# A decoder step on one core: the sample's closing sums, projection banks, cached-memory key steps and decode pacing

## The chip, the cores and the metric

One program runs on one core of a Trainium2 chip, in one launch. The metric is the device time of an execution in microseconds (us). The engines named below are TensorE (PE, with its weight loads PEld), VectorE (DVE), ScalarE (ACT), GpSimd (POOL) and SyncE (SP). POOL, ACT and SP also issue DMA transfers, each from its own queue.

## What is computed

One inference step of a decoder layer for two groups of rows that share the weights: a prompt of 1024 rows and a sample of 8 rows, one per sequence, width 1024, all in fp32. The sample attends to 8192 cached positions per sequence through a page table. In short:

```python
q, k, v, logf, u, z = mixer_inputs(rmsnorm(xs, g_mix), w_in, b_f, g_sgu_v)
att = fox_sample(q, k, v, logf, cache_k, cache_v, cache_logf, page_table)
xs = xs + merge_heads(att, sgu_sample(u, z, w_s, b_s), g_att_out, g_sgu_out, w_o)
xs = xs + cross_attend(rmsnorm(xs, g_cross), cache_mem_k, cache_mem_v, w_cq, w_co)
f, conv_s = conv_ffn(rmsnorm(xs, g_ffn), state_conv, w_up, conv_w, conv_b, w_down)
y_sample = rmsnorm(xs + f, g_final)
```

The prompt goes through the same layer with causal attention over its own rows, cross-attention into 256 memory tokens, and the same gated feed-forward block (width 2816, twice for gate and value). Outputs are both groups' results and the new keys, values, gates, memory keys and values and convolution states.

## The kernel before

**Two programs in one.** `prompt()` and `sample()` are Python generators that record instructions. `prompt()` yields an estimate of TensorE time after each piece of work. The loop at the end of `build` adds these estimates to `acc` and takes the next step of `sample()` whenever `acc` reaches the figure that `PACE` holds for the current phase. The phases of the prompt are p1 (projections), att0 and att1 (attention of the two halves of the rows), mid0 and mid1 (output projection and cross-attention of a half), ffn0 and ffn1 (its feed-forward block). While the sample is in its decode part, the figure is the prompt phase's; behind decode it is that of `rest`. After the recording, a scheduler with a timeline of its own orders the instructions of each engine; each engine then runs its queue strictly in that order and waits on semaphores.

**The prompt.** Its products are written as three fp32r matmuls each (high times high, high times low, low times high; lines 246 to 248, 410 to 412, 973 to 975). Weights come in 512 KB loads on SP's queue, and ACT and DVE split each into its high and low part (lines 209 and 210). Product tiles take PSUM banks from two rings, `ba` (four banks) and `bb` (two), in turns through `BK()`. In the feed-forward block DVE empties a bank with lines 1194 and 1195, and line 1226 adds a down-projection's product to the residual.

**The sample.** Each of its matrix products has 8 rows, so its weights are the moving operand and four products stand side by side in the 32-column groups of one bank (line 258, `sample_mm`; lines 1371, 1568, 1614 and 1653 for values, memory values, up- and down-projection). A product with a selection matrix (`selS`, lines 1465 and 1666) then sums the four groups into 8 rows. It has two banks of its own, `ms` and `dv`, one each, and four buffers `kv` of 1 MB, filled on POOL's queue, for everything that it loads: cached keys and values (lines 1306 and 1365), weights (1474, 1610, 1648) and cached memory (1531, 1564).

**The rest of the sample behind decode** (`sample_rest`): closing the attention, then `sample_proj` with `w_o`, a norm, `sample_proj` with `w_cq`, whose result goes through a DRAM tensor `q2s_d` and comes back broadcast to all partitions; the key steps of the cached memory, one for each of eight sequences (two multiplications, line 1535, and a reduction, line 1536, on DVE); softmax; the memory's values; `sample_proj` with `w_co`; the up-projection (22 steps of 1 MB), the down-projection (11 steps of 1 MB into `ys`, one `dv` and one `ms` bank), the closing sums (line 1666, in banks from `BK()`), the final norm and the store of `o_ys`.

**Order by hand.** `behind(e)` records an instruction so that the scheduler issues it after the newest prompt instruction of engine `e` at that point; decode's DVE and PE steps use it (lines 1310 and 1369).

Of the kernel before, what the change touches and what calls it, by code (L numbers as in the profile page):

```python
# [11 lines left out]
AF = mybir.ActivationFunctionType  # L12
ALU = mybir.AluOpType
AX = mybir.AxisListType
PSUM = bass.MemoryType.PSUM
ENG = mybir.EngineType
DRAM = bass.MemoryType.DRAM

P = 128
# [10 lines left out]
FF = 2816  # L30
NF = FF // P
NPAGE = 64
EPS = 1e-6
NEG = -1e30
UW = 1024
# [37 lines left out]
KS = 2  # L73
BKQ = 1
LA = (2, 2)
PACE = {'p1': 7.0, 'att0': 20.0, 'mid0': 8.0, 'ffn0': 8.5, 'att1': 15.0, 'mid1': 6.8, 'ffn1': 2.5, 'rest': 2.9}


def build(nc, tc, ctx, a, phases=None):
# [13 lines left out]
    def nm(s):  # L93
        cnt[0] += 1
        return f"{s}_{cnt[0]}"
# [13 lines left out]
    def KV():  # L109
        return dpool.tile([P, 2048], F32, tag="kv", bufs=NKV, name=nm("kv"))  # L110

    def sm(shape, tag, bufs=2, dt=F32):
        return small.tile(shape, dt, tag=tag, bufs=bufs, name=nm(tag))

    def BA():
        return psum.tile([P, 512], F32, tag="ba", bufs=4, name=nm("ba"))

    def BB():
        return psum.tile([P, 512], F32, tag="bb", bufs=2 + MB, name=nm("bb"))
# [3 lines left out]
    def BK():  # L123
        turn_[0] += 1
        return BB() if turn_[0] % BR == BR - 1 else BA()
# [3 lines left out]
    def MS():  # L129
        return BB() if MB else psum.tile([P, 512], F32, tag="ms", bufs=1, name=nm("ms"))  # L130

    def DV():
        return psum.tile([P, 512], F32, tag="dv", bufs=1, name=nm("dv"))

    def D2(n=512, dt=F32):
        return dpool.tile([P, 512], dt, tag="d2", bufs=5, name=nm("d2"))[:, :n]
# [5 lines left out]
    mmul = nc.tensor.matmul  # L142
# [12 lines left out]
    selS = cp[:, C_SELS : C_SELS + 8]  # L155
# [6 lines left out]
    epsb = const.tile([P, 1], F32, tag="epsb", name="epsb")  # L162
    nc.vector.memset(epsb, EPS)
    warm = const.tile([P, 1], F32, tag="warm", name="warm")
# [28 lines left out]
    def rstd_of(ssq, n, width, tag):  # L193

        p = ssq.shape[0]
        r = sm([P, width], tag + "r", 2)[:p]
        nc.vector.tensor_scalar(r, ssq, 1.0 / n, EPS, op0=ALU.mult, op1=ALU.add)
        nc.gpsimd.tensor_tensor(r, r, mhalf[:p, :width], op=ALU.pow)
# [54 lines left out]
    def sample_mm(ps, raw, kk, xT, n, off=0):  # L253

        for q in range(2):
            k = kk * 2 + q
            j = k % 4
            mmul(
                ps[32 * j : 32 * j + 32, :n],
                xT[:, k, :],  # L260
                raw[:, q, off : off + n],
                start=(k < 4),
                stop=(k >= 4),
                tile_position=(0, 32 * j),
            )
# [43 lines left out]
    def p1(early):  # L309
# [25 lines left out]
        def stats(hf):  # L335
# [9 lines left out]
            for dst, m in ((rstd8, 64.0), (rstd, 1.0)):  # L345
                v = sm([P, 4], "xv", 2)
                nc.vector.tensor_scalar(v, ssx[:, c], m / D, m * EPS, op0=ALU.mult, op1=ALU.add)
                nc.gpsimd.tensor_tensor(dst[:, c], v, mhalf[:, :4], op=ALU.pow)
# [898 lines left out]
    bgs, acc, phase = [], [0.0], ["p1", None]  # L1247

    def behind(e):

        return tc.issue_after(last[e]) if e in last else nullcontext()
# [208 lines left out]
    def sample_out(n, ps, fin):  # L1460
        t = D2()
        nc.scalar.activation(t, ps, AF.Copy)
        yield 1
        ps2 = MS()
        mmul(ps2[:8, :], selS, t, start=True, stop=True)
        fin(n, ps2[:8, :])

    def sample_proj(w, xT, fin):
        for n in range(2):
            ps = MS()  # L1470
            for kk in range(4):
                if kk % 2 == 0:
                    raw = KV().rearrange("p (k n) -> p k n", n=512)
                    nc.gpsimd.dma_start(raw, w[kk * 256 : (kk + 2) * 256, n * 512 : (n + 1) * 512].rearrange("(k p) n -> p k n", p=P))
                    yield 1
                sample_mm(ps, raw[:, (kk % 2) * 2 : (kk % 2) * 2 + 2, :], kk, xT, 512)
            yield from sample_out(n, ps, fin)

    def sample_rest(xs):
        yield 1  # L1480
# [31 lines left out]
        def add(n, ps):  # L1512
            nc.vector.tensor_tensor(xs[n], ps, xs[n], op=ALU.add)

        yield from sample_proj(a["w_o"], xsT, add)
        yield from sample_norm(xs, gp[:, G_CROSS : G_CROSS + 8], xsT)
        q2s = pair("s")

        def toq(n, ps):
            nc.vector.tensor_scalar(q2s[n], ps, 1.0 / 16, None, op0=ALU.mult)  # L1520
            nc.sync.dma_start(q2s_d[:, n * 512 : (n + 1) * 512], q2s[n])

        yield from sample_proj(a["w_cq"], xsT, toq)

        sS = sm([P, 2, 8, 4], "sS", 1)
        for b in range(8):
            qb = [D2(), D2()]
            for n in range(2):
                nc.gpsimd.dma_start(qb[n], q2s_d[b : b + 1, n * 512 : (n + 1) * 512].broadcast_to((P, 512)))
            kv = KV()  # L1530
            nc.gpsimd.dma_start(kv.rearrange("p (a c) -> p a c", c=D), a["cmk"][b].rearrange("(a p) c -> p a c", p=P))
            kvv = kv.rearrange("p (a c) -> p a c", c=D)
            for n in range(2):
                kn = kvv[:, :, n * 512 : (n + 1) * 512]
                nc.vector.tensor_tensor(kn, kn, qb[n].unsqueeze(1).broadcast_to((P, 2, 512)), op=ALU.mult)
            nc.vector.tensor_reduce(sS[:, :, b, :], kv.rearrange("p (a h d) -> p a h d", a=2, h=4), axis=AX.X, op=ALU.add)
            yield 1
        yield 1
        tr = MS()
        for mt in range(2):  # L1540
# [21 lines left out]
        for b in range(8):  # L1562
            kv = KV().rearrange("p (a c) -> p a c", c=D)
# [11 lines left out]
            op=ALU.mult,  # L1575
# [3 lines left out]
        for n in range(2):  # L1579
            ps = MS()  # L1580
# [3 lines left out]
        sample_T(y, ones[:, 0:8], xsT)  # L1584
        yield 1
        yield from sample_proj(a["w_co"], xsT, add)
        yield from sample_norm(xs, gp[:, G_FFN : G_FFN + 8], xsT)

# [14 lines left out]
        for f4 in range(11):  # L1603
            ps = DV()
            for q in range(2):
# [6 lines left out]
                for k in range(8):  # L1612
# [5 lines left out]
                        start=(k < 4),  # L1618
                        stop=(k >= 4),
# [3 lines left out]
            t = D2()  # L1623
# [21 lines left out]
        ys = [DV(), MS()]  # L1645
        for f2 in range(0, NF, 2):
            raw = KV().rearrange("p (f d) -> p f d", f=2)
            nc.gpsimd.dma_start(raw, a["w_down"][f2 * P : (f2 + 2) * P, :].rearrange("(f p) d -> p f d", p=P))
            for q in range(2):
                f = f2 + q  # L1650
                j = f % 4
                for n in range(2):
                    mmul(
                        ys[n][32 * j : 32 * j + 32, :],
                        g[:, f * 8 : f * 8 + 32],
                        raw[:, q, n * 512 : (n + 1) * 512],
                        start=(f < 4),
                        stop=(f >= NF - 4),
                        tile_position=(0, 32 * j),
                    )  # L1660
            yield 1
        for n in range(2):
            t = D2()
            nc.scalar.activation(t, ys[n], AF.Copy)
            ps = BK()
            mmul(ps[:8, :], selS, t, start=True, stop=True)
            add(n, ps[:8, :])
        r = rms8(xs)
        for n in range(2):
# [85 lines left out]
    def sample():  # L1755
        yield from decode()
        phase[1] = "rest"
        yield from sample_rest(pair("dec"))
# [4 lines left out]
    for t in prompt():  # L1763
        ins = nc.cur_bb.bb.instructions
        for e in (ENG.DVE, ENG.PE):
            for i in range(len(ins) - 1, max(seen, len(ins) - 400) - 1, -1):
                if ins[i].engine == e:
                    last[e] = ins[i]
                    break
        acc[0] += t  # L1770
        most = int(t / PACE[phase[1] or phase[0]]) + 1
        while bgs and not held[0] and most and acc[0] >= PACE[phase[1] or phase[0]]:
            most -= 1
            acc[0] -= PACE[phase[1] or phase[0]]
            if next(bgs[0], None) is None:
                bgs.pop()
        seen = len(nc.cur_bb.bb.instructions)
    for _ in bgs.pop() if bgs else ():
        pass
# [90 lines left out]
```

## Time and profile before

| | |
|---|---|
| median of 3 runs | 1930.2 us (1928.2 to 1940.83) |
| the profiled execution | 1933.38 us, of which span 1931.6 us |
| mean granted TensorE clock in it | 0.972 of full speed |
| DMA | 517.07 MB, mean 268 GB/s over the span |
| cached keys and values, POOL's queue | 128 + 128 loads of 1 MB |
| PE busy / DVE busy in 1500 to 1600 | 100.00 / 54.17 us |
| PE busy / DVE busy in 1600 to 1700 | 92.47 / 73.93 us |

The profile is one execution, recorded by the hardware profiler. All positions in time are microseconds from the span's start. Busy times of PE are modelled, since matmuls are pipelined: distances from start to start tell more than lengths. A matmul of plain fp32 (the sample's) appears as two records, one of fp32r as one. "Waits" give, for an idle engine, what it waited for by the last semaphore. The times of decode in it: its last value products stand at about 1490, and the rest of the sample runs from there to 1866, the prompt to the end.

### The profile page before, as it was taken

To read this page: it belongs to the slowest core of one execution; us is meant where nothing else is said; L and a number is where in the kernel's file an instruction comes from. 1 tells how busy PE (TensorE), PEld (TensorE's weight loads), DVE (VectorE), ACT (ScalarE), POOL (GpSimd) and SP (SyncE) were. 2 spreads that over 40 slices of the span, in tenths; PEclk is the share of its full clock that TensorE was granted. 3 is DMA by queue.
4 is the path that set the end of the run, shared out by engine and by line. 5 is a ranking of instruction groups with operands and counts; after the bars stand their busy time and mean duration, and the time that the engine had idled before them with its cause. 6 is when DMAs were issued, how large, how long until landed. Compare 5 with 4: busy or idle time off the path is not lost.

```text
span 1931.6 us, 24224 instructions
## 1 busy us (share of the span) xinstructions
PE 1821.0 (94%) x9255; PEld 1300.7 (67%) x9255; DVE 1403.6 (73%) x1662; ACT 760.8 (39%) x1435; POOL 475.3 (25%) x429
## 2 busy tenths in 40 slices
PE   8999989778898999999999999998999998999798
PEld 5987667555676667777767776675665776667456
DVE  4888668777687786989989899888764459553134
ACT  5332356566632535333333233335353333332122
POOL 1322232322123232223331323343312012101200
PEclk9999999899999999999999999998999998999899
DMA  8877988744496875869787889888769467767841
GB/s 322 288 240 274 332 316 294 255 154 144 158 358 242 317 291 196 304 258 347 283 310 289 312 294 362 322 325 308 282 259 344 163 205 252 290 174 290 332 156 65
DMA packets 156372, 517.07 MB, mean 268 GB/s; under 512 B 20168, under 2 KB 41928, under 8 KB 123488
## 3 DMA queue, kind: packets, MB, share of 16 engines
q0 software_dynamic: 56400, 339.04, 47.1%
q1 hardware_dynamic: 92944, 163.89, 24.4%
q10 hardware_dynamic: 6912, 12.59, 1.7%
q8 instruction: 73, 1.20, 0.2%
q14 instruction: 43, 0.35, 0.1%
HBM read 493.63 MB, written 21.84 MB: 267 GB/s over the span
## 4 chain that ended last, share of the span: by engine, by line
PE 64%; DVE 7%; DMA 4%; ACT 3%; issue 2%; POOL 0%; DVEq 0%; POOLq 0%; ACTq 0%; SPq 0%
PE ba L246 9%; PE ba L247 9%; PE ba L248 9%; PE bb L246 5%; PE bb L247 5%; PE bb L248 5%; PE dv L1371 5%; DMA kv<-cache_k,kidx 2%; DVE kv L1312 1%; DMA kv<-w_down 1%; DVE s L1316 1%; PE ba L973 1%; PE ba L975 1%; PE ba L974 1%; PE dv L1614 1%
## 5 line engine op out<-in xcount | busy, mean ns | idle before, releaser
L209 ACT ACTIVATE wh<-wr 128x1024 fp32r<-128x1024 f32 (+2 forms) x220 | 228.8, 1044 | 474.9 <-PE ba L247 147.1
L210 DVE TENSOR_TENSOR wl<-wr,wh 128x1024 fp32r<-128x1024 f32 (+2 forms) x220 | 262.4, 1200 | 146.0 <-PE ba L248 60.6
L1312 DVE TENSOR_TENSOR kv<-kv,d 128x2048 f32<-128x2048 f32 (+1 forms) x139 | 292.4, 2114 | 33.9 <-DMA kv<-cache_k,kidx 31.9
L1306 POOL DMA_INDIRECT kv<-cache_k,kidx x128 | 179.6, 1403 | 556.0 <-DVE s L1316 251.0
L1316 DVE TENSOR_REDUCE s<-kv 128x32 f32<-128x2048 f32 (+1 forms) x139 | 292.1, 2106 | 0.6
L1365 POOL DMA_INDIRECT kv<-cache_v,kidx x128 | 176.2, 1376 | 419.1 <-PE dv L1371 162.4
L246 PE MATMUL ba<-wh,u 128*128 128x512 f32 (+1 forms) x591 | 224.2, 381 | 0.0
L247 PE MATMUL ba<-wl,u 128*128 128x512 f32 (+1 forms) x591 | 223.8, 379 | 0.0
L248 PE MATMUL ba<-wh,u 128*128 128x512 f32 (+1 forms) x591 | 220.8, 378 | 0.5 <-DVE u L210 0.5
L246 PE MATMUL ba<-u,wh 128*128 128x512 f32 (+2 forms) x528 | 206.7, 392 | 1.3 <-DVE u L213 1.2
L247 PE MATMUL ba<-u,wh 128*128 128x512 f32 (+2 forms) x528 | 207.3, 393 | 0.0
L248 PE MATMUL ba<-u,wl 128*128 128x512 f32 (+2 forms) x528 | 206.3, 391 | 0.0
L1371 PE MATMUL dv<-kv,s 128*32 128x512 f32 x1024 | 135.8, 609 | 4.8 <-DMA kv<-cache_v,kidx 4.8
L246 PE MATMUL bb<-u,wh 128*128 128x512 f32 (+2 forms) x336 | 134.9, 401 | 2.2 <-DVE u L213 2.2
L247 PE MATMUL bb<-u,wh 128*128 128x512 f32 (+2 forms) x336 | 133.3, 397 | 2.5 <-DVE u L213 2.5
L248 PE MATMUL bb<-u,wl 128*128 128x512 f32 (+2 forms) x336 | 132.6, 395 | 0.0
L246 PEld LDWEIGHTS ba<-wh,u 128*128 128x128 f32 x591 | 111.3, 188 | 30.1 <-issue 7.1
L248 PEld LDWEIGHTS ba<-wh,u 128*128 128x128 f32 x591 | 110.8, 188 | 26.7 <-issue 4.6
L247 PEld LDWEIGHTS ba<-wl,u 128*128 128x128 f32 x591 | 111.3, 188 | 22.7 <-issue 2.1
L246 PEld LDWEIGHTS ba<-u,wh 128*128 128x128 f32 x528 | 100.3, 190 | 32.9 <-issue 8.0
L247 PEld LDWEIGHTS ba<-u,wh 128*128 128x128 f32 x528 | 100.5, 190 | 31.9 <-issue 11.3
L248 PEld LDWEIGHTS ba<-u,wl 128*128 128x128 f32 x528 | 100.4, 190 | 28.6 <-issue 8.9
(419 smaller groups left out, 3124.1 us busy)
## 6 DMA issues: line engine op xcount, KB each, us to landing
wr<-w_up SPq DMA_DIRECT2D x88, 512.0 KB
kv<-w_up POOLq DMA_DIRECT2D x22, 1024.0 KB
wr<-w_down SPq DMA_DIRECT2D x40, 512.0 KB
kv<-w_down POOLq DMA_DIRECT2D x11, 1024.0 KB
wr<-w_in SPq DMA_DIRECT2D x16, 512.0 KB
wr<-w_o SPq DMA_DIRECT2D x16, 512.0 KB
wr<-w_cq SPq DMA_DIRECT2D x16, 512.0 KB
wr<-w_co SPq DMA_DIRECT2D x16, 512.0 KB
```

The lines of the kernel that those rows point to most:

```text
L209: nc.scalar.activation(h, src, AF.Copy)
L210: nc.vector.tensor_tensor(l, src, h.bitcast(F32), op=ALU.subtract)
L246: mmul(out, sh, mh, start=(i == 0), stop=False)
L247: mmul(out, sh, ml, start=False, stop=False)
L248: mmul(out, sl, mh, start=False, stop=(i == n - 1))
L973: mmul(pss[i], mh[k][:, tb], wh, start=(k == korder[0]), stop=False)
L974: mmul(pss[i], mh[k][:, tb], wl, start=False, stop=False)
L1306: nc.gpsimd.indirect_dma_start(kv, None, a["cache_k"], off(kidx[:, b, ch : ch + 1]))
L1312: nc.vector.tensor_tensor(kvv[:, i : i + m, :], kvv[:, i : i + m, :], qb.unsqueeze(1).broadcast_to((P, m, 512)), op=ALU.mult)
L1316: nc.vector.tensor_reduce(s[:, ch * 4 + i : ch * 4 + i + m, :].rearrange("p k h -> p (k h)"), kvv[:, i : i + m, :].rearrange("p k (h d) -> ...
L1365: nc.gpsimd.indirect_dma_start(kv, None, a["cache_v"], off(kidx[:, b, ch : ch + 1]))
L1371: mmul(dv[32 * j : 32 * j + 32, :], s[:, ch * 4 : ch * 4 + 4, :].rearrange("p k h -> p (k h)"), kvv[:, j, :], start=(ch == 0), stop=(ch == ...
```

## The change

- `PACE`: mid0 8.0 to 8.3, ffn0 8.5 to 8.8, mid1 6.8 to 7.2 (decode's steps are taken less often there), rest 2.9 to 2 (the rest's steps more often).
- `sample_proj`: the two halves of the columns take `dv` and `ms` in turns instead of `ms` twice; both halves' products come first, then both sums, each in the bank that its half had. One step fewer is yielded for each projection.
- The key steps of cached memory: DVE's part is recorded inside `behind(ENG.DVE)`, and the reduction over both halves of the memory is written as two.
- The closing sums: both banks `ys` are copied out first, and the sums take `dv` and `ms` instead of banks from `BK()`.
- The loop's step may yield a weight `w`, which takes `w` times the pace; every yield is 1 here (`CMK` = 1), so this does nothing as it stands.

```diff
-PACE = {'p1': 7.0, 'att0': 20.0, 'mid0': 8.0, 'ffn0': 8.5, 'att1': 15.0, 'mid1': 6.8, 'ffn1': 2.5, 'rest': 2.9}
+PACE = {'p1': 7.0, 'att0': 20.0, 'mid0': 8.3, 'ffn0': 8.8, 'att1': 15.0, 'mid1': 7.2, 'ffn1': 2.5, 'rest': 2}
...
     def sample_out(n, ps, fin):
         t = D2()
         nc.scalar.activation(t, ps, AF.Copy)
         yield 1
-        ps2 = MS()
+        ps2 = (DV, MS)[n]()
         mmul(ps2[:8, :], selS, t, start=True, stop=True)
         fin(n, ps2[:8, :])
 
     def sample_proj(w, xT, fin):
+        outs = []
         for n in range(2):
-            ps = MS()
+            ps = (DV, MS)[n]()
             for kk in range(4):
...
                 sample_mm(ps, raw[:, (kk % 2) * 2 : (kk % 2) * 2 + 2, :], kk, xT, 512)
-            yield from sample_out(n, ps, fin)
+            outs.append(sample_out(n, ps, fin))
+            next(outs[n])
+        for o in outs:
+            yield from o
+        yield 1
...
-            for n in range(2):
-                kn = kvv[:, :, n * 512 : (n + 1) * 512]
-                nc.vector.tensor_tensor(kn, kn, qb[n].unsqueeze(1).broadcast_to((P, 2, 512)), op=ALU.mult)
-            nc.vector.tensor_reduce(sS[:, :, b, :], kv.rearrange("p (a h d) -> p a h d", a=2, h=4), axis=AX.X, op=ALU.add)
-            yield 1
+            with behind(ENG.DVE):
+                for n in range(2):
+                    kn = kvv[:, :, n * 512 : (n + 1) * 512]
+                    nc.vector.tensor_tensor(kn, kn, qb[n].unsqueeze(1).broadcast_to((P, 2, 512)), op=ALU.mult)
+                for i in range(2):
+                    nc.vector.tensor_reduce(sS[:, i, b, :], kvv[:, i, :].rearrange("p (h d) -> p h d", h=4), axis=AX.X, op=ALU.add)
+            yield CMK
...
+        ts = [D2(), D2()]
         for n in range(2):
-            t = D2()
-            nc.scalar.activation(t, ys[n], AF.Copy)
-            ps = BK()
-            mmul(ps[:8, :], selS, t, start=True, stop=True)
+            nc.scalar.activation(ts[n], ys[n], AF.Copy)
+        for n in range(2):
+            ps = (DV, MS)[n]()
+            mmul(ps[:8, :], selS, ts[n], start=True, stop=True)
             add(n, ps[:8, :])
...
-            if next(bgs[0], None) is None:
+            w = next(bgs[0], None)
+            if w is None:
                 bgs.pop()
+            else:
+                acc[0] -= (w - 1) * PACE[phase[1] or phase[0]]
```

More of the change, by code (lines that the diff above doesn't have):

```diff
@@ L32 @@
 NPAGE = 64
+CMK = 1
 EPS = 1e-6
```

## The prediction

> **What bounds the kernel now.** I read the page's parts 1 and 4 first, then stages, then TensorE's own order in time.
>
> ```profile
> PE 1821.0 (94%) x9255; PEld 1300.7 (67%) x9255; DVE 1403.6 (73%) x1662; ACT 760.8 (39%) x1435; POOL 475.3 (25%) x429
> ...
> PE 64%; DVE 7%; DMA 4%; ACT 3%; issue 2%; POOL 0%; DVEq 0%; POOLq 0%; ACTq 0%; SPq 0%
> ```
>
> TensorE is busy 94% of the span and carries 64% of the chain of waits. Both kernels issue the same matmuls, so the change can only move time in which TensorE stands still, or the cost of switching between prompt and sample. I therefore looked for places where no prompt matmul runs. The stages around the largest one (columns: length, then busy time of PE, PEld, DVE, ACT, POOL, then granted clock, DMA share, GB/s):
>
> ```profile
> 1755.20:1805.00 49.80, 49.80 (x374) 35.02 (x373) 15.05 (x19) 13.11 (x20) 8.76 (x13) 1.00 0.90 325
> 1805.00:1855.80 50.80, 35.55 (x219) 12.68 (x218) 4.21 (x8) 5.87 (x11) 9.27 (x13) 0.80 0.82 320
> 1855.80:1906.60 50.80, 50.80 (x218) 40.42 (x218) 27.93 (x43) 17.76 (x32) 0.56 (x1) 1.00 0.16 54
> 1906.60:1931.60 25.00, 17.26 (x75) 13.66 (x73) 12.34 (x23) 6.20 (x17) 2.17 (x4) 0.92 0.21 85
> ```
>
> In 1805 to 1855.8 PE is busy 35.55 of 50.80 us at a granted clock of 0.80, while DMA moves 320 GB/s. The 50.8 us behind it have PE full and DMA nearly idle at 54 GB/s. PE's order in time shows what that hole is (start, length, instructions merged; brackets: idle before and its releaser):
>
> ```profile
> 1804.67 0.40 PE L248 MATMUL ba<-u,wl 128*128 128x512 f32 x1
> 1805.00 1.07 PE L1614 MATMUL dv<-kv,xsT 128*32 128x256 f32 x16
> 1806.00 1.06 PE L1629 MATMUL ms<-cp,d 128*128 128x8 f32 x8
> 1806.99 1.07 PE L1614 MATMUL dv<-kv,xsT 128*32 128x256 f32 x16
> ...
> 1825.26 1.96 PE L1653 MATMUL dv<-kv,d 128*32 128x512 f32 x8 [2.53 <-issue]
> 1826.94 1.96 PE L1653 MATMUL ms<-kv,d 128*32 128x512 f32 x8
> ...
> 1834.63 1.06 PE L1653 MATMUL dv<-kv,d 128*32 128x512 f32 x4 [3.39 <-DMA kv<-w_down]
> ...
> 1849.28 1.93 PE L1653 MATMUL dv<-kv,d 128*32 128x512 f32 x4 [2.49 <-DMA kv<-w_down]
> ...
> 1854.86 1.02 PE L1666 MATMUL bb<-d,cp 128*8 128x512 f32 x2 [0.76 <-ACT d L1664]
> ...
> 1855.81 0.50 PE L246 MATMUL bb<-u,wh 128*128 128x512 f32 x1
> ```
>
> From 1804.67 to 1855.81 there is only sample work: the end of its up-projection, all of its down-projection, its first closing sum (L1666), and directly behind that sum the prompt's next matmul. The sum's bank comes from BK, the prompt's own ring. In the old program order 109 sample matmuls stand in one run here; elsewhere the longest run is 20. The rows name loads of `w_down` as what PE waits for.
>
> **Part 1, the closing sums.** The hole is 1855.81 − 1804.67 − 0.23 (one prompt matmul) = 50.9 us. The work in it, start to start at full rate: 6 blocks L1614 at 1.00, 4 of L1629 at 0.99, 11 steps L1653 at 1.68, the sum 0.95: 6.0 + 4.0 + 18.5 + 0.95 = 29.4. So 21.5 us are waits and half-rate matmuls. With the sums in DV and MS, the new program order has no run over 20 sample matmuls: the last up steps, a block of 16 and seven blocks of 4 in the down-projection, and the sums stand between prompt matmuls. That costs switching:
>
> ```profile
> 1481.81 0.39 PE L246 MATMUL ba<-u,wh 128*128 128x512 f32 x1
> 1482.13 1.06 PE L1371 MATMUL dv<-kv,s 128*32 128x512 f32 x8
> 1483.13 0.51 PE L247 MATMUL ba<-u,wh 128*128 128x512 f32 x1
> 1483.47 0.40 PE L248 MATMUL ba<-u,wl 128*128 128x512 f32 x1
> ```
>
> A block of 8 takes 1483.47 − 1481.81 − 2 × 0.23 = 1.20 us, of which 0.86 is its own (16 take 0.86 more), so 0.34 a switch. The new order has about 11 more switches in this stretch: 3.7 us. Do the loads keep up? The chain shows the steady spacing ahead of the hole, and SyncE the sample's last store:
>
> ```profile
> 1792.66 1.00 PE dv L1614 x16
> ...
> 1800.94 1.00 PE dv L1614 x16
> ...
> 1864.69 0.99 SPq L1674 DMA_DIRECT2D o_ys<-dec  x2
> ```
>
> Two sample steps of 1 MB each stand every 8.3 us, in the old order to 1805 and in the new one to the end of the up-projection. A `kv` buffer is reused four steps later, so a load has two spacings less its own pair (16.6 − 3) = 14 us of PE work to hide in, and at that spacing PE was full from 1755 to 1805. In the hole, at 1.0 to 1.7 us a step, it had 4 to 7. In the new down-projection the order leaves it 14 us or more. Over 1755 to 1907 DMA moved 49.8 × 325 + 50.8 × 320 + 50.8 × 54 = 35.2 MB, 233 GB/s when spread; so I take no wait. Part 1: −21.5 + 3.7 = **−17.8 us**; bounds −21.5 (no switch cost) and −4 (14 us of the waits stay). From the first closing sum to the sample's last store it took 1865.7 − 1854.86 = 10.8 us; behind the second sum the new order still has 82 prompt matmuls, 18.9 us, so this ending stays covered. A sum now waits for ACT's copy out of its own bank (0.76 us in the row of L1666), with prompt matmuls queued behind it; the new order puts some ahead of it too, so I take none of that.
>
> **Part 2, key steps of cached memory.** Sixteen multiplications stay; eight reductions become sixteen halves. DVE's rows in 1575 to 1645, and the nearest half-size reduction:
>
> ```profile
> L1535 DVE TENSOR_TENSOR kv<-kv,d 128x1024 f32<-128x1024 f32 x16 | 19.3, 1219 | 5.2 <-DMA d<-q2s_d 5.2
> L1536 DVE TENSOR_REDUCE sS<-kv 128x8 f32<-128x2048 f32 x8 | 18.2, 2280 | 0.0
> L210 DVE TENSOR_TENSOR wl<-wr,wh 128x1024 fp32r<-128x1024 f32 x10 | 12.2, 1220 | 2.3 <-PE ba L248 2.3
> L1194 DVE SCALAR_TENSOR_TENSOR t<-ba,gp,t 128x511 f32<-128x511 f32 x5 | 3.7, 745 | 0.4 <-ACT hlast L1193 0.4
> L1195 DVE SCALAR_TENSOR_TENSOR t<-ba,gp,t 128x510 f32<-128x510 f32 x5 | 3.7, 740 | 0.0
> L1201 DVE TENSOR_TENSOR t<-t,t 128x512 f32<-128x512 f32 x3 | 2.1, 687 | 0.0
> L210 DVE TENSOR_TENSOR u<-t,u 128x512 fp32r<-128x512 f32 x3 | 2.1, 687 | 0.0
> L1197 DVE TENSOR_TENSOR t<-t,fix 128x2 f32<-128x2 f32 x8 | 1.2, 151 | 0.0
> ...
> L1316 DVE TENSOR_REDUCE s<-kv 128x16 f32<-128x1024 f32 x22 | 26.3, 1208 | 0.1
> ```
>
> The split itself: 8 × (2 × 1.208 − 2.280) = 1.1 us of DVE. [...] Today these steps cost PE a stall:
>
> ```profile
> 1620.87 0.40 PE L248 MATMUL ba<-wh,u 128*128 128x512 f32 x1
> 1628.23 0.77 PE L246 MATMUL bb<-wh,u 128*128 128x512 f32 x1 [6.97 <-DVE t L1197]
> 1628.80 0.63 PE L247 MATMUL bb<-wl,u 128*128 128x512 f32 x1
> ```
>
> PE waits 7 us for a bank that DVE empties late, then runs at half rate (0.57 instead of 0.23 apart). Counting DVE work from the first key step to what PE needs: in the old order up to a `wl`, 16 × 1.219 + 7 × 2.280 of sample and 8 × 1.220 + 7 × (0.745 + 0.740 + 0.151) + 3 × 0.687 + 2 × 0.687 of prompt = 60.1 us, against 235 matmuls × 0.23 = 54.1 of PE: 6 late. In the new order the key steps stand closer together, at the end of an up-projection group: up to the `u` that the down-projection needs, 16 × 1.219 + 14 × 1.208 + 5 × 1.220 + 3 × 1.636 + 4 × 0.687 = 50.1 us against 175 × 0.23 = 40.3: 9.8 late. So queueing behind the prompt does not remove the stall (on POOL only four of the `q2s_d` and `cmk` issues change places); I take **+4 us**, between −7 (stall gone) and +12 (both DMA waits of 5.2 us on top, at half clock).
>
> **Part 3, banks in turns and the rest at pace 2.** Each projection's 16 products stand in one block, not two of 8: three switches fewer, −1.0 us. The rest starts later (by program order, decode's last value product stands 44 us of prompt work further on) and catches up by its pace; the steps of this rest that stood at 1755 to 1805 left PE full at the old spacing, and denser they could wait for their loads, so I take 0, from −2 to +6.
>
> **Part 4, decode wider in the middle stages.** This removes and adds no work. What it can touch are two stalls:
>
> ```profile
> 1177.24 0.66 PE L860 MATMUL ba<-cp,u 128*128 128x128 f32 x4
> 1181.69 1.12 PE L860 MATMUL ba<-cp,u 128*128 128x128 f32 x4 [3.80 <-DVE u L932]
> ...
> 1319.29 0.60 PE L1098 MATMUL bb<-cp,u 128*128 128x128 f32 x4
> 1324.70 1.94 PE L1371 MATMUL dv<-kv,s 128*32 128x512 f32 x8 [4.81 <-DMA kv<-cache_v,kidx]
> ...
> 1321.66 2.29 DVE L1312 TENSOR_TENSOR kv<-kv,d 128x2048 f32<-128x2048 f32 x1 [5.88 <-DMA kv<-cache_k,kidx]
> ```
>
> The second is DVE and PE both waiting for cache loads in a stretch crowded with transfers; a step per 7.2 instead of 6.8 eases it by 6% of the sample's traffic. With the half rate behind it that stall is worth some 8 us, of which I take half, −4. Ahead of the first, the new order has one cached key step more on DVE (about 2 us): +2. Together −2, between −10 (both gone) and +6.
>
> **Sum.** −17.8 + 4 − 1 − 2 = −16.8 us. The profiled execution took 1933.38 us (span 1931.6), 3.2 over the median 1930.2. 1933.4 − 16.8 = 1916.6 for that execution, 1913.4 against the median; I say **1913**.
>
> **Rivals.** (a) The middle gains too: both stalls of part 4 go, 3.80 + 4.81 = 8.6 us. With the key stall left, −17.8 + 4 − 1 − 8.6 = −23.4, 1907; with that gone as well (−7), −34, 1896; about 1902. For it: slower decode leaves transfers more room. Against: the count in part 2, and that 6% is little.
>
> (b) The tail stays bound by transfers: the hole ran at 320 GB/s, near the 325 of the stretch ahead, so the loads may only move their wait between prompt matmuls. Residual 14 us: −4 − 1 + 4 − 2, about 1927. Against: 54 GB/s behind the hole.
>
> (c) DVE becomes the bound in the key steps and gives most back: +12 in place of +4, middle +6: −17.8 + 12 + 6 − 1 = −1, 1929. For it: 9.8 us late even with no transfer late.
>
> (d) Slower: the key steps, now placed right behind the prompt's newest DVE instruction, hold DVE's queue while their loads have not landed, and the prompt's bank evictions (L1194, L1195) behind them hold PE. To end over 1% slower (19.3 us) this must cost 17.8 + 19.3 = 37 us, so 4.6 us for each of eight steps; then 1950. For it: the 5.88 us wait above. Against: sixteen multiplications waited 5.2 us in all.
>
> (e) The change does not do what it says, the closing run stays: the new program order excludes it.
>
> On (b): the row has a granted clock of 0.80 over the hole, whose waits shown are 3.39 us or less. [...]
>
> **How the numbers follow.** The sum as worked out 0.38, (a) 0.24, (b) 0.15, (c) 0.15, (d) 0.08. 1% is 19.3 us, so 1910.9 is the bound; 1% is about what a measurement of this kernel tells from no change. The forecast lies 2 us above it: of its 0.38 I give 0.16 to faster; with (a) that is 0.40. Slower 0.08; the rest, 0.52, within 1%. Range 1895 to 1928: from (a)'s middle down 7 us to just past (b); it leaves out part of (c), (d) and the far end of (a). The forecast alone has 1905 to 1921.
>
> **What would show it.** Right: prompt matmuls throughout 1800 to 1860 with no DMA wait over 1 us, DMA near 230 GB/s there; L1653 in blocks of 8 and 32 records; a PE stall of 8 to 14 us at the key steps. Wrong: L1614 or L1653 still waiting for `kv` loads (b); no key stall (a); DVE waits for `cmk` or `q2s_d` loads of several us per step (c, d).

## The result and the profile after

| | median | runs | ratio to before, 95% interval |
|---|---|---|---|
| before | 1931.75 us | 13 | |
| changed | 1918.4 us | 13 (1911.56 to 1925.27) | 0.9924 (0.9907 to 0.9942) |

The change takes 0.76%, some 14 us, off the time: inside the forecast's range, on the side that was forecast, 5 us behind its figure. The profiled execution has a span of 1916.7 us, 14.9 less than the one before. Of the 12 executions of the experiment called e2 below, one took 3534.83 us, a slow run that its ratio leaves out.

Parts 1 and 4 of the changed kernel's page (busy time, and the chain that ended last):

```profile
PE 1815.8 (95%) x9255; PEld 1300.0 (68%) x9255; DVE 1404.5 (73%) x1670; ACT 758.9 (40%) x1435; POOL 471.7 (25%) x429
...
PE 82%; DVE 7%; DMA 4%; issue 3%; ACT 3%; POOL 1%; SPq 0%; DVEq 0%; POOLq 0%; ACTq 0%
```

TensorE has as many matmuls as before. Its 82% of the chain can't be set against the 64% of before, which the prediction read as TensorE's share: the shares of before add up to 80% only, because that chain could be followed back no further than to 372 us. The shares of DVE, DMA and ACT are the same in both. The stages that answer to the hole of before (length, busy PE, PEld, DVE, ACT, POOL, clock, DMA share, GB/s):

```profile
1755.20:1805.00 49.80, 49.80 (x377) 35.30 (x377) 14.77 (x18) 12.77 (x17) 8.73 (x13) 1.00 0.89 327
1805.00:1855.80 50.80, 50.80 (x331) 36.47 (x331) 23.87 (x36) 18.01 (x32) 7.95 (x12) 1.00 0.80 271
1855.80:1890.00 34.20, 34.20 (x139) 16.92 (x137) 10.71 (x18) 6.58 (x12) 2.14 (x3) 1.00 0.47 174
```

PE is busy throughout at full clock, and the transfers that were pressed into the hole now run on to 1890. In the groups of the whole span the sample's up- and down-projection (now lines 1622 and 1661; figures behind the bar: busy, mean, then idle time ahead of them) wait for nothing:

```profile
L1622 PE MATMUL dv<-kv,xsT 128*32 128x256 f32 x352 | 23.3, 385 | 0.0
L1661 PE MATMUL dv<-kv,d 128*32 128x512 f32 x44 | 9.6, 604 | 0.0
L1661 PE MATMUL ms<-kv,d 128*32 128x512 f32 x44 | 9.4, 592 | 0.0
```

PE's order in time, the last step of the down-projection and the closing sums:

```profile
1880.75 0.40 PE L247 MATMUL ba<-wh,u 128*128 128x512 f32 x1
1881.08 1.06 PE L1661 MATMUL dv<-kv,d 128*32 128x512 f32 x4
1881.96 1.03 PE L1661 MATMUL ms<-kv,d 128*32 128x512 f32 x4
1882.92 0.50 PE L248 MATMUL ba<-wl,u 128*128 128x512 f32 x1
...
1888.19 1.02 PE L1675 MATMUL dv<-d,cp 128*8 128x512 f32 x2
1889.05 1.02 PE L1675 MATMUL ms<-d,cp 128*8 128x512 f32 x2
1890.00 0.51 PE L249 MATMUL bb<-wh,u 128*128 128x512 f32 x1
```

Each block has prompt matmuls on both sides and none has a wait in brackets. The stall that grew with the change stands 230 us earlier. The rows with a wait in PE's order, and the half-rate matmuls behind the longest (idle time and its releaser in brackets):

```profile
1631.53 0.50 PE L247 MATMUL ba<-wh,u 128*128 128x512 f32 x1 [0.28 <-ACT u L210]
...
1635.53 0.50 PE L247 MATMUL ba<-wh,u 128*128 128x512 f32 x1 [1.87 <-DVE t L1196]
...
1638.98 0.50 PE L248 MATMUL ba<-wl,u 128*128 128x512 f32 x1 [1.58 <-DVE wl L211]
...
1649.51 0.80 PE L247 MATMUL ba<-wh,u 128*128 128x512 f32 x1 [3.60 <-ACT u L210]
1650.10 0.63 PE L248 MATMUL ba<-wl,u 128*128 128x512 f32 x1
1650.53 0.63 PE L247 MATMUL ba<-wh,u 128*128 128x512 f32 x1
...
1656.22 0.72 PE L249 MATMUL ba<-wh,u 128*128 128x512 f32 x2 [1.22 <-DVE u L211]
```

Before, the key steps cost PE one long wait of 6.97 us (7.5 from 1550 to 1700 in all); now they cost these five, together 8.55 us (10.4 in all), and again one stretch at half rate (0.43 from start to start instead of 0.23). The rows name ACT and three different DVE lines, but the stage shows one engine behind them (columns as above):

```profile
1631.00:1660.00 29.00, 18.77 (x64) 12.62 (x62) 29.00 (x31) 5.03 (x6) 5.36 (x9) 0.88 0.74 260
```

DVE is busy for 29.00 of 29 us and ACT for 5.03: ACT's `u` at L210 rounds a gate product for which ACT itself had waited: the idle time ahead of that copy, 12.55 us, ended with DVE's L1202.

### The profile page after: what moved, and what is told of

It reads as the page before. It is cut to its first block, busy times and chain, and to the rows that moved or that the text cites. A ratio compares the mean times of both kernels' runs of the same rounds, so it can differ in the third digit from the quotient of the medians.

```text
span 1916.7 us, 24252 instructions
## 1 busy us (share of the span) xinstructions
PE 1815.8 (95%) x9255; PEld 1300.0 (68%) x9255; DVE 1404.5 (73%) x1670; ACT 758.9 (40%) x1435; POOL 471.7 (25%) x429
## 4 chain that ended last, share of the span: by engine, by line
PE 82%; DVE 7%; DMA 4%; issue 3%; ACT 3%; POOL 1%; SPq 0%; DVEq 0%; POOLq 0%; ACTq 0%
PE ba L247 12%; PE ba L249 12%; PE ba L248 12%; PE bb L247 7%; PE bb L248 7%; PE bb L249 7%; PE dv L1372 6%; DVE kv L1313 1%; PE dv L1622 1%; PE ba L974 1%; PE ba L976 1%; PE ba L975 1%; PE bb L773 1%; DVE sS L1544 1%; PE ba L729 1%
## 5 line engine op out<-in xcount | busy, mean ns | idle before, releaser
L210 ACT ACTIVATE wh<-wr 128x1024 fp32r<-128x1024 f32 (+2 forms) x220 | 228.2, 1043 | 507.3 <-PE ba L248 163.2
L1307 POOL DMA_INDIRECT kv<-cache_k,kidx x128 | 171.0, 1336 | 508.4 <-DVE s L1317 206.0
L247 PE MATMUL ba<-wh,u 128*128 128x512 f32 (+1 forms) x596 | 228.5, 384 | 6.3 <-ACT u L210 4.1
L249 PE MATMUL ba<-wh,u 128*128 128x512 f32 (+1 forms) x596 | 224.6, 380 | 1.2 <-DVE u L211 1.2
L248 PE MATMUL ba<-u,wh 128*128 128x512 f32 (+2 forms) x520 | 203.9, 392 | 0.2 <-DVE u L214 0.2
L247 PE MATMUL ba<-u,wh 128*128 128x512 f32 (+2 forms) x520 | 203.6, 393 | 0.0
L247 PE MATMUL bb<-u,wh 128*128 128x512 f32 (+2 forms) x344 | 138.7, 403 | 2.2 <-DVE u L214 2.2
L248 PE MATMUL bb<-u,wh 128*128 128x512 f32 (+2 forms) x344 | 136.7, 397 | 2.6 <-DVE u L214 2.6
```

What stands on the lines that cost most here:

```text
L210: nc.scalar.activation(h, src, AF.Copy)
L247: mmul(out, sh, mh, start=(i == 0), stop=False)
L248: mmul(out, sh, ml, start=False, stop=False)
L249: mmul(out, sl, mh, start=False, stop=(i == n - 1))
L1307: nc.gpsimd.indirect_dma_start(kv, None, a["cache_k"], off(kidx[:, b, ch : ch + 1]))
```

## The experiments

Times are medians in us; each ratio is to the kernel before, run on the same chip beside it. Chips differ: the kernel before took 1928.97 beside the first four, 1934.0 beside the next four, 1934.09 beside the last four. So figures from different chips are compared by ratio.

| | what it is | median | ratio (95%) |
|---|---|---|---|
| e1 | before + closing sums | 1908.9 | 0.9899 (0.9876 to 0.9921) |
| e2 | changed, key steps undone | 1916.85 | 0.9932 (0.9910 to 0.9954) |
| e3 | changed, old PACE | 1909.94 | 0.9901 (0.9878 to 0.9923) |
| e4 | changed, projections undone | 1927.52 | 0.9992 (0.9974 to 1.0009) |
| e5 | changed, closing sums undone | 1974.12 | 1.0219 (1.0197 to 1.0241) |
| e6 | changed, mid1 undone | 1911.75 | 0.9900 (0.9875 to 0.9925) |
| e7 | changed, half of the key work | 1903.56 | 0.9850 (0.9829 to 0.9871) |
| e8 | old PACE, half of the sums on ACT | 1900.53 | 0.9830 (0.9809 to 0.9852) |
| e9 | changed, again | 1919.82 | 0.9928 (0.9901 to 0.9954) |
| e10 | changed, half of the sums on ACT | 1906.4 | 0.9867 (0.9843 to 0.9892) |
| e11 | as e8, again | 1902.94 | 0.9852 (0.9822 to 0.9882) |
| e12 | old PACE, all sums on ACT | 1901.42 | 0.9841 (0.9812 to 0.9869) |

### The closing sums, alone and undone

e1 is the kernel before with this edit only:

```diff
+        ts = [D2(), D2()]
         for n in range(2):
-            t = D2()
-            nc.scalar.activation(t, ys[n], AF.Copy)
-            ps = BK()
-            mmul(ps[:8, :], selS, t, start=True, stop=True)
+            nc.scalar.activation(ts[n], ys[n], AF.Copy)
+        for n in range(2):
+            ps = (DV, MS)[n]()
+            mmul(ps[:8, :], selS, ts[n], start=True, stop=True)
             add(n, ps[:8, :])
```

> The kernel before with the closing sums alone moved to DV and MS behind both copies (no other edit). Theory (the closing run was the loss): the run of 109 sample matmuls falls apart into blocks of 20 or fewer, PE's order elsewhere stays, so 21.5 us of waits and half clock go and about 4 us of switches come: 14 to 22 us faster than before, no kv wait over 1 us behind 1800. Rival (the tail is bound by its transfers): the waits only move between prompt matmuls, 4 us faster or less. Second rival (other parts of the change carry the gain): less than half of the change's 14 us.

It is 1.0% faster than before, 20 us: more than the whole change brings. By the program order, PE's first 7674 of 8073 instructions, up to the old hole, are the same in both, so one matmul of the prompt serves as an anchor. In the trace of before it is the row at 1804.67, from which 1931.6 − 1804.67 = 126.9 us are left. In e1's order in time it is

```profile
1801.31 0.39 PE L248 MATMUL ba<-u,wl 128*128 128x512 f32 x1
```

with 1906.2 − 1801.31 = 104.9 left. The edit is worth **22.0 us** from there on; the other 3.4 of the two spans' difference arose ahead of it, where the order is the same. The hole of 50.9 us has become 28.9 us of PE time. Its pieces, in e1's order in time:

```profile
1838.76 1.08 PE L1653 MATMUL dv<-kv,d 128*32 128x512 f32 x8
1839.64 1.06 PE L1653 MATMUL ms<-kv,d 128*32 128x512 f32 x8
1840.50 1.08 PE L1653 MATMUL dv<-kv,d 128*32 128x512 f32 x8
...
1842.37 0.50 PE L247 MATMUL ba<-u,wh 128*128 128x512 f32 x1
...
1849.89 1.06 PE L1653 MATMUL dv<-kv,d 128*32 128x512 f32 x4
1850.77 1.03 PE L1653 MATMUL ms<-kv,d 128*32 128x512 f32 x4
1851.74 0.50 PE L246 MATMUL bb<-u,wh 128*128 128x512 f32 x1
```

The block of 32 records holds four steps and takes 1842.37 − 1838.76 = 3.61 us, 0.90 a step. A step alone, 8 records, takes 1851.74 − 1849.89 = 1.85, up to the prompt's next matmul. I had put all eleven at 1.68, a spacing read inside the hole. The clock does not make the difference, as it is 1.00 here for both; the block does: eight records of `dv` take 0.88 from start to start in the block of four steps, and four records take 0.88 in the step alone.

e5 undoes the same edit in the changed kernel.

> The changed kernel with the closing sums back in banks from BK, each right behind its copy. In its program order 265 sample matmuls then stand in one run: the whole up- and down-projection of the sample, 33 steps of 1 MB. Theory (the prompt's ring holds the prompt back until the sum, and the run lasts as long as its loads): 33 MB at the 320 GB/s of the old hole are 103 us, PE's own work in it about 52, some 11 us of switches saved: 35 to 55 us slower than the changed kernel, 1953 to 1973. Rival (once the rest runs at its new place, the bank of the sums hardly matters): 1915 to 1922.

It comes out 56 us slower than the changed kernel by the medians and 2.2% slower than before; at the top of what was expected, a little past it. The sum's bank is thus the cause, and with decode ending later the old form would have cost 2.5 times what it cost before. The run in e5 is even longer than the 265 matmuls expected: the projection with `w_co` stands in it too, 300 sample matmuls in all. Two of its rows in time, and a stage out of the run:

```profile
1726.64 1.93 PE L1622 MATMUL dv<-kv,xsT 128*32 128x256 f32 x16 [6.06 <-DMA kv<-w_up]
1729.29 1.94 PE L1622 MATMUL dv<-kv,xsT 128*32 128x256 f32 x16 [0.72 <-ACT d L1632]
...
1740.00:1760.00 20.00, 17.73 (x136) 9.14 (x124) 0.00 (x0) 1.79 (x3) 4.30 (x6) 0.50 0.96 354
```

DVE does nothing (0.00 of 20 us): the prompt stands still as a whole while PE works through the sample's up-projection at a clock of 0.50, with 0.96 of the DMA engines' time taken.

### The key steps

e2 records them as before in the changed kernel:

```diff
-            with behind(ENG.DVE):
-                for n in range(2):
...
-                for i in range(2):
-                    nc.vector.tensor_reduce(sS[:, i, b, :], kvv[:, i, :].rearrange("p (h d) -> p h d", h=4), axis=AX.X, op=ALU.add)
-            yield CMK
+            for n in range(2):
...
+            nc.vector.tensor_reduce(sS[:, :, b, :], kv.rearrange("p (a h d) -> p a h d", a=2, h=4), axis=AX.X, op=ALU.add)
+            yield 1
```

> The changed kernel with the key steps recorded as before: not behind DVE, one reduction per step instead of two halves. Theory: the order of DVE's instructions around them is the same, so only the split's 8 x (2 x 1.208 - 2.280) = 1.1 us of DVE go, in a stretch where PE waits for DVE: 0 to 2 us faster than the changed kernel. Rival (queueing behind the prompt's DVE work costs or gains by itself): 4 us or more of difference, either way.

0.9932 against 0.9924 and 0.9928: no difference that these intervals can show. The edit itself does next to nothing. In the program order, a kernel with `behind` and one reduction and a kernel without `behind` have the same sequence on every engine, so queueing behind the prompt changes nothing there; what is left is the split. Its price stands in the groups of the changed kernel, 1600 to 1662, DVE:

```profile
L1542 DVE TENSOR_TENSOR kv<-kv,d 128x1024 f32<-128x1024 f32 x16 | 19.2, 1216 | 1.7 <-DMA d<-q2s_d 1.6
L1544 DVE TENSOR_REDUCE sS<-kv 128x4 f32<-128x1024 f32 x16 | 18.7, 1207 | 0.0
```

18.7 us for sixteen halves against 18.2 for eight whole ones: 0.5 us, where I had 1.1. The row's mean counts the overlap of neighbours twice (16 × 1.207 = 19.3); the busy time of the group (18.7) does not.

The stall is another matter. e7 removes half of DVE's work and leaves every load:

```diff
+        nc.vector.memset(sS, 0.0)
...
-                for n in range(2):
+                for n in range(1):
                     kn = kvv[:, :, n * 512 : (n + 1) * 512]
...
-                    nc.vector.tensor_reduce(sS[:, i, b, :], kvv[:, i, :].rearrange("p (h d) -> p h d", h=4), ...
+                    nc.vector.tensor_reduce(sS[:, i, b, 0:2], kvv[:, i, :512].rearrange("p (h d) -> p h d", h=2), ...
```

> The changed kernel with half of the key steps' DVE work left out: only the first 512 columns are multiplied and summed, the loads all stay. DVE's work per step goes from about 4.8 to 2.4 us, 18 us in all. Theory (PE's stall there is DVE's count, 50.1 us of work against 40.3 of matmuls): 31.6 against 40.3, so the waits of 10 us from 1631 to 1660 and the half clock behind them (2 us) go: 9 to 13 us faster than the changed kernel, 1905 to 1909. Rival (the loads of q2s_d and cached memory hold DVE's queue): less than 4 faster.

0.9850 against 0.9924: 14 us, the 10.4 us of waits and the half rate behind them, and a little more than was expected. The stage 1550 to 1700, first the kernel before, then the changed one, then e7 (three views):

```profile
1550.00:1700.00 150.00, 142.47 (x638) 102.29 (x637) 104.88 (x136) 49.21 (x76) 23.17 (x36) 0.97 0.69 246
```

```profile
1550.00:1700.00 150.00, 139.56 (x642) 96.31 (x641) 102.62 (x141) 48.63 (x79) 28.23 (x42) 0.98 0.71 256
```

```profile
1550.00:1700.00 150.00, 150.00 (x705) 105.33 (x704) 95.69 (x149) 53.96 (x87) 28.25 (x42) 1.00 0.74 273
```

PE idles 7.5 us before, 10.4 changed, 0 with half of the work, at a higher DMA rate than either. The rival that late loads hold DVE's queue falls: the loads were all there, and the stall was not. What DVE itself waited for among the changed kernel's key steps was little, once PE and once a load, as its order in time shows:

```profile
1609.17 1.23 DVE L211 TENSOR_TENSOR wl<-wr,wh 128x1024 fp32r<-128x1024 f32 x1 [1.28 <-PE ba L249]
...
1613.31 1.23 DVE L1542 TENSOR_TENSOR kv<-kv,d 128x1024 f32<-128x1024 f32 x1 [1.59 <-DMA d<-q2s_d]
```

### The pace of decode

e3 puts the four old figures back, e6 only mid1's:

```diff
-PACE = {'p1': 7.0, 'att0': 20.0, 'mid0': 8.3, 'ffn0': 8.8, 'att1': 15.0, 'mid1': 7.2, 'ffn1': 2.5, 'rest': 2}
+PACE = {'p1': 7.0, 'att0': 20.0, 'mid0': 8.0, 'ffn0': 8.5, 'att1': 15.0, 'mid1': 6.8, 'ffn1': 2.5, 'rest': 2.9}
```

Of e3 this was expected:

> The changed kernel with all four old figures of PACE (mid0 8.0, ffn0 8.5, mid1 6.8, rest 2.9). My prediction gave the middle stages -2 us, so undoing would lose 2 (1920). Rival from the two traces (PE's excess over full-rate spacing rose by 6 us from 600 to 1400 and fell by 4 behind it): the wider decode costs 2 to 4, and undoing gains it (1914 to 1916). Second rival (rival (a) of the prediction, the middle gains): undoing loses 8 us or more.

and of e6:

> The changed kernel with mid1 alone back at 6.8. All four old figures gave 8.5 us. Theory 1 (decode in mid1 is what costs: PE's excess over full-rate spacing was 6.6 us higher from 1150 to 1400, of which 4.3 came back by 1500): 2 to 4 faster than the changed kernel, 1914 to 1916. Theory 2 (what costs is that decode ends 165 prompt matmuls later and crowds the key steps; here it ends 42 earlier, a quarter): 0 to 2 faster, 1916 to 1918.

("Excess" in these texts: for each matmul the distance to the next start, less the usual distance of such a pair.) e3 is faster than e2, on the same chip, by 6.9 us, and of e2's executions all but three took longer than the slowest of e3's six (1913.07). Its ratio is 0.9901 against 0.9924 for the changed kernel, and those two intervals overlap. The first rival was right in sign and low in size. mid1 alone has the same ratio as all four (0.9900), more than either theory had for it, though decode then ends only a quarter of the way earlier (42 of 165 prompt matmuls); but its interval holds the changed kernel's 0.9924 as well, so that mid1 alone gives it all back is not shown. The figure for the rest moves nothing: with 2.9 or 2 the program order of every engine is the same. e3 is also the kernel e1 with the new projections and key steps, and on the one chip the two differ by 1.0 us (1909.94 and 1908.9): what the whole change loses against e1 comes with the new figures of PACE.

Where does it go? Not into the two stalls that I had named. PE's waits in the changed kernel, the first row in mid0, the others in mid1:

```profile
674.30 0.66 PE L1065 MATMUL bb<-cp,t 128*128 128x128 f32 x4 [3.93 <-DMA t<-o_mk]
...
1179.17 1.07 PE L1372 MATMUL dv<-kv,s 128*32 128x512 f32 x8 [1.28 <-DMA kv<-cache_v,kidx]
...
1183.41 0.66 PE L861 MATMUL ba<-cp,u 128*128 128x128 f32 x4 [2.59 <-DVE u L933]
1185.28 1.12 PE L861 MATMUL bb<-cp,u 128*128 128x128 f32 x4 [1.21 <-DVE u L214]
...
1329.34 1.99 PE L1081 MATMUL ba<-t,u 128*128 128x256 f32 x8 [2.81 <-ACT t L1069]
...
1342.03 2.07 PE L1107 MATMUL ba<-u,t 128*128 128x512 f32 x2 [2.80 <-ACT u L1100]
```

The 3.80 for DVE became 2.59 and two others, together 5.08; the 4.81 for the cache loads went, and two waits for ACT came, 5.61. PE is busy 334.44 of 350 us from 1150 to 1500, against 334.73 before: the stalls moved, their sum did not. The wait at 674.30 is new. There the prompt reads its own memory keys back from DRAM, and PE waits for that load; e7, e9 and e10, with the same figure for mid0, have this wait too (4.5, 4.2 and 4.3 us), and in the kernel before the same matmul, at 668.56, waits for nothing. e6 keeps that figure; its trace gains elsewhere, PE being busy 337.10 us from 1150 to 1500, and 144.50 us from 1550 to 1700 against the changed kernel's 139.56.

### The projections

e4 puts `sample_proj` back (both halves in MS, each half's sum behind its products):

```diff
-            ps = (DV, MS)[n]()
+            ps = MS()
...
-            outs.append(sample_out(n, ps, fin))
-            next(outs[n])
-        for o in outs:
-            yield from o
-        yield 1
+            yield from sample_out(n, ps, fin)
```

> The changed kernel with sample_proj as before (both halves in MS, each half's sum right behind its products, one step more yielded each). In its program order the rest of the sample then ends behind the prompt's last matmul: the end of the up-projection, all 11 steps of the down-projection and the closing, 70 sample matmuls, have no prompt work beside them. Theory (the banks in turns are what lets the rest end in time once decode ends 44 us later): 11 MB at 320 GB/s are 34 us, the closing 10.8 us, of which some 19 us are PE's own work anyway: 20 to 40 us slower than the changed kernel, 1938 to 1958. Rival (my part 3: banks in turns are worth the three switches, 1 us): 1917 to 1922.

11 us slower than e2 on the same chip: neither figure. The trace holds two effects against each other (stages, then rows in time):

```profile
1600.00:1700.00 100.00, 100.00 (x443) 76.59 (x442) 81.01 (x99) 34.39 (x53) 17.25 (x28) 1.00 0.72 255
...
1870.20:1925.40 55.20, 27.64 (x145) 7.94 (x141) 11.22 (x24) 10.31 (x26) 10.83 (x15) 0.82 0.65 251
```

```profile
1870.26 0.49 PE L249 MATMUL ba<-wh,u 128*128 128x512 f32 x1
...
1888.03 1.42 PE L1656 MATMUL dv<-kv,d 128*32 128x512 f32 x4 [2.87 <-DMA kv<-w_down]
...
1907.12 1.02 PE L1670 MATMUL dv<-d,cp 128*8 128x512 f32 x2 [0.75 <-ACT d L1667]
```

The prompt's last matmul is at 1870.26, and the 55 us behind it have PE busy for 27.64: 27.6 us of idle time at the end. The changed kernel's own end, from 1890 to 1916.7, has 7.4, so e4 loses 20 more, the least that the theory had. But the key steps, at other prompt work, cost PE nothing (100.00 of 100 us from 1600 to 1700), which returns the 10.4 us of waits there; that leaves some 10 us, and the two spans differ by 8.7. So the banks in turns matter by the time at which the rest ends, not by three switches.

### Less for DVE: a faster kernel

If DVE's count is the stall, work can go to ACT, which stands at 40%. e8 and e11 (one kernel, with the old PACE), e10 (with the new) and e12 (both halves, with the old) let ACT take reductions over:

```diff
-                for i in range(2):
-                    nc.vector.tensor_reduce(sS[:, i, b, :], ...
+                nc.vector.tensor_reduce(sS[:, 0, b, :], ...
+            for h in range(4):
+                kh = kvv[:, 1, h * 256 : (h + 1) * 256]
+                nc.scalar.activation(kh, kh, AF.Copy, accum_out=sS[:, 1, b, h : h + 1])
```

Expected of e8:

> The changed kernel with the four old figures of PACE, and the second half of each key step's reduction taken from DVE to ACT (four copies with a running sum each, 32 in all). DVE gets 9.3 us less to do in the key steps. Theory (DVE's count is what makes PE late there, and ACT, busy 31 of 100 us, has room): 2 to 6 us faster than the same kernel with all reductions on DVE (1909.9), 1904 to 1908. Rival (the copies hold ACT's queue, in which the prompt's conversions and the last columns of the banks stand): 1910 to 1916.

Of e9, the changed kernel again:

> The changed kernel itself once more, on the same chip as the three kernels beside it: 0.992 of the kernel before, between 0.990 and 0.995.

Of e10:

> The changed kernel with its own PACE, and the second half of each key step's reduction on ACT. It tells where the new PACE costs its 4 to 7 us. Theory 1 (in the key steps, which stand closer together when decode ends later): 9.3 us less on DVE bring its count from 50.1 to 40.8 against PE's 40.3, the stall goes, 9 to 13 us faster than the changed kernel, and no more than 3 us slower than the same edit under the old figures. Theory 2 (in the middle stages): faster than the changed kernel too, but at least 4 us slower than the same edit under the old figures.

Of e11:

> The kernel with the old figures of PACE and the second half of each reduction on ACT, again, beside the others on one chip: 0.981 to 0.986 of the kernel before.

Of e12:

> As the kernel beside it, with both halves of each reduction on ACT: 64 copies with a running sum, no reduction left on DVE (9.4 us less again). Theory (the DVE stall is gone with the first half; PE's excess over full-rate spacing in 1550 to 1650 was 4 us, against 12 under DVE alone): within 2 us of it. Rival 1 (some of the stall is left): 2 to 5 faster. Rival 2 (64 copies of ACT in 50 us hold the prompt's conversions in ACT's queue): 3 or more slower.

e9 repeats the result (0.9928). e10 is 13.4 us faster than e9 beside it (0.9867), so the stall was DVE's count. The copies' price in e8, from ACT's groups at 1540 to 1625:

```profile
L1546 ACT ACTIVATE kv<-kv 128x256 f32<-128x256 f32 x32 | 13.0, 410 | 6.8 <-DVE kv L1542 5.5 <-ACT hlast L1194 1.3
...
L1546 ACT ACTIVATION_READ_ACCUMULATOR kv<-kv 128x1 f32 x32 | 6.0, 189 | 0.0
```

19 us of ACT and 6.8 of waiting take 9 us off DVE: a bad exchange by the busy time of the engines, and a good one for the kernel. e8 and e11, one kernel twice, are at 0.983 and 0.985, some 14 and 9.5 us below e3's ratio. That is more than the 2 to 6 that were expected, and more than the 4.2 us that PE idles in e3's key steps; where the rest comes from is not shown. The second half (e12, 0.9841) adds nothing that shows. e10 is 3.5 us slower than e11, between the 3 of theory 1 and the 4 of theory 2, and their intervals overlap. The stages fit both in part: from 550 to 1150, PE is busy 584.3, 583.5 and 583.7 us with the new figures (changed, e9, e10) and 585.4, 585.6 and 585.8 with the old (e3, e8, e11), so about 2 us go in mid0 and ffn0, where the new wait at 674.30 stands; from 1550 to 1700 e3 has 145.78 against the changed kernel's 139.56, so more went in the key steps. How the rest divides is not settled by these runs.

## Why the prediction came out, point by point

- **Part 1, the closing sums** (−17.8 taken): the right mechanism, too small. By the anchor it is −22.0. I had 29.4 us of work and 3.7 of switches, 33.1; it takes 28.9. The mis-sized term is the hole's own work: 11 × 1.68 = 18.5 us for the down-projection took one price for every step, while four steps in one block take 0.90 each and one alone 1.85, the way to the prompt included, an estimated 4 × 0.90 + 7 × 1.85 = 16.6 with part of the switches in it. Short blocks have to be priced by their length, from rows that stand as they will stand. The loads kept up; no `kv` wait is left, and rival (b) falls. They did not spread as evenly as I had it: 271 GB/s from 1805 to 1855.8 and 174 behind, not near 230.
- **Part 2, key steps** (+4, between −7 and +12): as forecast in place and cause. The count said 9.8 us late; the waits in the trace are 8.55 us. PE's idle time from 1550 to 1700 grew by 2.9 us, and the half rate did not grow (granted clock 0.97 before, 0.98 after; its spacing is 0.43 in both, the 0.57 of the prediction being that of the first pair). That the count came so near is in part luck. It added durations, and neighbours on DVE overlap: from start to start a multiplication or half reduction takes 1.13 us, and the same 50.1 come to an estimated 46. Against that, DVE stood idle for some 3 us among them, 1.28 for PE and 1.59 for `q2s_d`, which the count had at nothing. The split was over-priced (18.7 − 18.2 = 0.5, not 1.1). Part of the whole key stall, 14 us by e7, was there before the change.
- **Part 3, projections** (−1): right with the old PACE, where e3 and e1 differ by 1.0 us. With the new PACE it was mis-read: undone, the projections cost 11 to 13 us (e4 against e2 and against the changed kernel), 20 more at the end less what the key steps get back. And the rest does not catch up "by its pace": its figure moves no instruction; the banks do it.
- **Part 4, decode wider** (−2, between −10 and +6): wrong in sign. The four figures cost 4.4 us by the ratios (0.9924 − 0.9901 = 0.23%) to 6.9 by the medians of one chip. The step that failed is "of which I take half, −4": I credited a named stall with going, and others took its place, so that PE's idle time from 1150 to 1500 stayed (15.3 us before, 15.6 after). I did not count the wait for `o_mk` in mid0, 3.9 us, and I priced the key steps' new place in part 2 without seeing that this pace had put them there.
- **The sum**: −16.8 taken, −14 measured. −22 for part 1 and +8 for the rest (e1 against e2, one chip) were taken as −17.8 and +1: two errors of opposite sign. That the figure is nearer than its steps is luck.
- **Rivals**: (a) falls, since the middle gains nothing; (b) falls; (c) was half right, as DVE binds in the key steps, at 14 us in all but with only some of that new; (d) falls with e7, and in the changed kernel loads held DVE's queue for only some 1.6 us at the key steps; (e) was excluded and did not come.

## What to carry to other kernels

A result of a background task that takes a buffer from the foreground's ring ties the foreground to everything queued ahead of it (here 22.0 us in the kernel before, 56 in e5); look for the one long run without foreground work, and see what its last instruction allocates. Where one engine's backlog stalls another, count its work between two points that the other needs, and ask whether a half-idle third engine can take a piece even at twice the price (in e8 19 us of ACT for 9 of DVE; e10 is 13.4 us faster than e9). A stall that a retiming is to remove should be credited only if it is known what is late next (PE's idle time from 1150 to 1500 was 15.3 us before and 15.6 after).

## What the runs showed of the hardware

TensorE's clock did not come back in e5 for some 60 us: after one wait of 6.06 us it stood at 0.50 from 1727 to 1790, though the waits listed between, up to 1788, were 0.72 to 0.80 us each and PE was busy 17.73 of 20 us in the stage shown, with some 5.6 us of unbroken matmuls between waits (1729.29 to the next at 1735.70, which waited 0.80). A block of 16 took 1.94 us here instead of the 1.07 at 1718.52. How much longer the run became by that is not shown, since the loads took 0.96 of the DMA engines' time beside it. In the changed kernel, with the prompt's matmuls behind the key steps' wait of 3.60 us, the half rate lasted from 1649.51 to 1654.37 only (granted clock 0.50 from 1650 to 1654.4).

Executions of one order differ, too: over the first 550 us, where all these kernels have the same matmuls in the same order, PE's busy time lay between 494.7 (e11) and 502.5 us (e1). Differences of a few us between two single profiles are therefore read by anchors, not by spans.
